# Turning the accumulated modulation of the second layer on VectorE instead of TensorE, each step tied behind its block

## The chip, the cores and the metric

One core of a Trainium2 chip runs the whole program in one launch. The metric is the device time of that launch in microseconds, as the median of several runs; one further run was profiled, and all rows below come from it.

## The reference, cut to what matters

Two layers of a trunk over 512 latent and 256 context tokens of width 1024, all in float32. Each layer first makes six vectors of 1024 (shift, scale and gate for two sub-layers) for the latent tokens and six for the context tokens:

```
mx = silu(c)     @ w_ada[i] + b_ada[i]      # latent,  6 * 1024 numbers
mc = silu(c_ctx) @ w_ada[i] + b_ada[i]      # context, 6 * 1024 numbers
sx1, ax1, gx1, sx2, ax2, gx2 = split(mx, 6) # the same for mc
h = rmsnorm(x) * (1 + ax1) + sx1            # then projection, conv, attention, merge
x = x + gx1 * merged
x = x + gx2 * (square(relu(modulate(rmsnorm(x)) @ w_mlp1[i])) @ w_mlp2[i])
```

`w_ada[i]` is 1024 x 6144. The two products with it are what the change is about, for layer 1 (the second). They depend on nothing in layer 0, so they can be made at any time before layer 1 starts.

## The kernel before, in words

Activations lie with the 1024 features on partitions (8 blocks of 128) and the 768 tokens along the free axis. Every float32 product is made as three products of a high and a low part (`mm3`, lines 107 to 111: high by high, low by high, high by low); `split` (line 75) makes the parts, the high one on ScalarE, the low one on VectorE or GpSimd. `fm_block` (line 113) makes one block of 128 output features for a group of tokens: 24 products, with 512 columns for a latent block and 256 for a context block. Weights come in slabs of 256 output columns (`load_slab`, line 84): one load on the SP queue, then the split. Two raw buffers and two of each part hold slabs in the second half of a layer; a slab serves two latent and two context blocks.

The stage around the change is the MLP of layer 0 (lines 1196 to 1294). Four chunks `cch` of 1024 hidden features follow each other. In each, `hidden` (line 1211) makes the blocks `f` from the normed input `h2h`, `h2l`: relu and square on ScalarE, then the low part `fl` by a subtraction on VectorE (line 1219). Then `out_slabs` (line 1153) makes the blocks `r` with the second weight, and `residual` (line 1137) adds each to the stream `X` on VectorE (line 1140), reading PSUM. Ahead of the MLP the same `out_slabs` made the output projection `o`, with a norm (`norm_mod`, line 305) after each half of the tokens: sums of squares, a product `nc_n`, a power on GpSimd, a diagonal `dg_n`, its product `nb_n` as broadcast, and then for each of eight feature blocks a product `nu_n` on VectorE, a shift on ScalarE (`h2h`) and a low part (`h2l`) on VectorE or GpSimd.

Layer 0 makes its own modulation with `ada_slab` (line 214), by products on TensorE in four column tiles. Layer 1's is made inside the MLP of layer 0 by the generator `ada_rows` (line 242). It goes over 24 pairs of steps; pair `s` makes 256 of the 6144 columns for both vectors. A step `n` has half of the 1024 rows in `ar`, a tile of 128 x 1024 numbers in the pool `araw` with one buffer, loaded on SP (line 247). The rows lie on partitions, so the sum over rows is first made over the four row blocks of a step with VectorE: a copy scaled by `cvec` on ScalarE for row block 0 (line 260), multiply-adds into the accumulator `a` of 128 x 512 for the others (line 263): six in an even step, eight in an odd one. Then the next load is issued, and the generator yields. After an odd step what is left is to add up the 128 partitions of `a`: four transposes on TensorE against the identity into a PSUM tile `adaps` (line 272), a reduce along the free axis on VectorE (line 275), which leaves 128 x 4 numbers, and the addition of `b_ada` (line 277) into `ad`. The accumulator comes from the tag `t2k` (four buffers), which the loads of `layer_params` use too.

`ada_step` (line 1205) moves the generator on by one step; a call of it is a tick below. It is called after each latent block of `f` (but for the last of a chunk, and, in the first chunk, only from the third slab on, since the first two slabs are walked in halves), and as `tick` after each latent block of `r`. Ahead of the last `out_slabs`, line 1238 runs what is left of it, and `ada_gain` (line 282) makes `A1` from columns 8 to 15 of `ad`. The PSUM tiles of latent blocks, of context blocks and of `adaps` come from pools of 2, 2 and 4.

What sets the order: the program is traced in the order of the code, and when it is built a planner gives each engine a fixed order of its instructions. It may move an instruction ahead of others when its inputs are ready earlier, as it did with the first steps of `ada_rows`. `tc.issue_after(ins)` ties the instructions traced inside it to stand behind `ins` on the engine of `ins`, and only those of that engine. The tag `dg` of `spool` (one buffer) is used for the diagonals of the norms and, in layer 0, by `ada_slab`.

Of the kernel before, what the change touches and what calls it, by code (L numbers as in the profile page):

```python
# [8 lines left out]
F32 = mybir.dt.float32  # L9
F32R = mybir.dt.float32r  # L10
AF = mybir.ActivationFunctionType
ALU = mybir.AluOpType
AX = mybir.AxisListType

P = 128
# [24 lines left out]
R_BADA, R_N1, R_N2, R_BG, R_BDW, R_LNG, R_LNB, R_ANG, R_C, R_CC, R_END = (  # L40
    0, 48, 56, 64, 80, 84, 88, 92, 93, 101, 109)
# [5 lines left out]
def f32(ap):  # L47
    return ap.bitcast(F32)
# [3 lines left out]
def trunk_kernel(  # L52
# [6 lines left out]
    nc = tc.nc  # L59
# [3 lines left out]
    cpool = ctx.enter_context(tc.tile_pool(name="cpool", bufs=1))  # L63
# [3 lines left out]
    spool = ctx.enter_context(tc.tile_pool(name="spool", bufs=2))  # L67
# [62 lines left out]
    nc.sync.dma_start(cst, consts[:, :C_COS])  # L130
    ident = cst[:, C_ID : C_ID + P]
    ones = cst[:, C_ONE : C_ONE + P]
    mhalf = cpool.tile([P, 8], F32, name="mhalf")
    nc.gpsimd.memset(mhalf, -0.5)

# [5 lines left out]
    state = {"behind": (), "turn": None}  # L141
# [100 lines left out]
    def ada_rows(i, L):  # L242


        def load(n):
            r = state["rp"].tile([P, KT // 2, 256], F32, tag="araw", bufs=1, name=f"ar{i}_{n}")
            nc.sync.dma_start(r, rows(w_ada[i], 256 * (n // 2), 256)[:, 4 * (n % 2) : 4 * (n % 2) + 4])
            return r

        r = load(0)  # L250
        for n in range(48):
            s = n // 2
            if n % 2 == 0:
                a = state["tp"].tile([P, 512], F32, tag="t2k", bufs=state["nt"], name=f"adaac{i}_{s}")
                a = a.rearrange("p (q n) -> p q n", q=2)
            for j in range(4):
                k = 4 * (n % 2) + j
                for q in range(2):
                    if k == 0:
                        nc.scalar.activation(out=a[:, q], in_=r[:, j], func=AF.Copy,  # L260
                                             scale=cvec[:, k, q : q + 1])
                    else:
                        nc.vector.scalar_tensor_tensor(  # L263
                            out=a[:, q], in0=r[:, j], scalar=cvec[:, k, q : q + 1], in1=a[:, q],
                            op0=ALU.mult, op1=ALU.add)
            if n < 47:
                r = load(n + 1)
            yield
            if n % 2:
                ps = state["mi"](f"adaps{i}_{s}")  # L270
                for m in range(4):
                    nc.tensor.transpose(ps[:, m * P : m * P + P],
                                        a[:, m // 2, m % 2 * P : m % 2 * P + P], ident)
                ad = L["ad"][:, :, 2 * s : 2 * s + 2]
                nc.vector.tensor_reduce(out=ad, in_=ps.rearrange("p (q m k) -> p q m k", q=2, m=2),
                                        axis=AX.X, op=ALU.add)
                nc.vector.tensor_tensor(
                    out=ad, in0=ad,
                    in1=L["cols"][:, R_BADA + 2 * s : R_BADA + 2 * s + 2].unsqueeze(1)
                    .to_broadcast([P, 2, 2]), op=ALU.add)  # L280

    def ada_gain(L, which, ks=slice(0, KT)):
        par, r0, nm = ((1, R_N1, "A1"), (4, R_N2, "A2"))[which]
# [72 lines left out]
    for t in range(NTT):  # L356
# [4 lines left out]
        if t == 1:  # L361
            L = layer_params(0)
# [17 lines left out]
    for t in range(NTT):  # L380
        xn = xns[t]
        nc.scalar.activation(out=xn, in_=xrs[t], func=AF.Square, accum_out=rs[:, t : t + 1])
        r = rs[:, t : t + 1]
# [9 lines left out]
    for s in range(2):  # L393
        nc.vector.tensor_tensor(
            out=cvec[:, :, s], in0=L["cols"][:, R_C + 8 * s : R_C + 8 * s + 8],
            in1=sg[:, 8 * s : 8 * s + 8], op=ALU.mult)
# [38 lines left out]
    for i in range(DEPTH):  # L435
# [5 lines left out]
        cols = L["cols"]  # L441
# [536 lines left out]
        for half, lst in ((1, ga), (0, gc)):  # L978
            for s in range(4):
# [6 lines left out]
                for m in range(2):  # L986
                    mb = 2 * s + m
                    t = g3(f"g{i}_{half}_{mb}")
                    lst[mb] = t
                    for g in groups:  # L990
                        W = g.stop - g.start
                        ps = ps_for(g, f"gt{i}_{half}_{mb}_{g.start}")
# [70 lines left out]
        for s in range(4):  # L1063
# [3 lines left out]
            for g in groups:  # L1067
                W = g.stop - g.start
                for m in range(2):
                    mb = 2 * s + m  # L1070
# [23 lines left out]
        for s in range(2):  # L1094
# [7 lines left out]
            for m in range(4):  # L1102
                mb = 4 * s + m
# [33 lines left out]
        def residual(mb, g, ps, gate):  # L1137
            W = g.stop - g.start
            s = int(g.start >= SEQ)
            nc.vector.scalar_tensor_tensor(  # L1140
                out=X[:, mb, g], in0=ps[:, :W], scalar=gate[:, s, mb : mb + 1], in1=X[:, mb, g],
                op0=ALU.mult, op1=ALU.add)

        def out_block(w, s, g, m, hidden, gate, nm, stats):
            mb = 2 * s + m
# [57 lines left out]
            hl = hpool.tile([P, KT, NT], F32R, tag="hl", name=f"h1l_{i + 1}")  # L1203

        def ada_step():
            if not last:
                next(ada_todo, None)

        for cch in range(4):
            fh, fl = [None] * KT, [None] * KT  # L1210
            def hidden(w, mb, m, g):
                W = g.stop - g.start
                ps = ps_for(g, f"f{i}_{cch}_{mb}_{g.start}")
                fm_block(ps[:, :W], w, m * P, lambda k: (h2h[:, k], h2l[:, k]), g)
                r = gp.tile([P, 512], F32, tag="ar", bufs=3, name=f"fr{i}_{cch}_{mb}_{g.start}")
                nc.scalar.activation(out=r[:, :W], in_=ps[:, :W], func=AF.Relu)
                nc.scalar.activation(out=fh[mb][:, g], in_=r[:, :W], func=AF.Square)
                nc.scalar.activation(out=r[:, :W], in_=r[:, :W], func=AF.Square)
                nc.vector.tensor_tensor(out=fl[mb][:, g], in0=r[:, :W], in1=f32(fh[mb][:, g]),
                                        op=ALU.subtract)  # L1220

            for mb in range(KT):
                fh[mb] = g3(f"fh{i}_{cch}_{mb}", F32R)
# [148 lines left out]
```

## Time and profile before

| what | value |
|---|---|
| median of 3 runs | 2361.62 us (2360.18 to 2363.51) |
| the profiled execution, whole | 2362.06 us |
| its span from first to last instruction | 2360.0 us |
| granted TensorE clock, mean | 0.987 |
| busy: TensorE, VectorE, ScalarE, GpSimd | 2288.2, 1468.9, 993.2, 684.2 us |
| chain of waits that ended last: TensorE, VectorE, ScalarE, GpSimd | 84%, 7%, 3%, 2% |

Shares are of the span. A busy time is the sum of an engine's instructions with overlaps counted once; TensorE's matmuls overlap each other, so the distance between two starts, not the duration of one, says what a matmul takes.

### The profile page before, as it was taken

The page shows a single profiled execution, that of the slowest core. Times are in us where ns is not written, and L with a number is a line of the kernel's source. Part 1 is how long each engine was busy: PE and PEld are TensorE (multiplying, and loading weights), DVE is VectorE, ACT ScalarE, POOL GpSimd, SP SyncE. Part 2 cuts the span into 40 slices and gives each one's busy share as a digit, 9 for nine tenths or more (in the row PEclk, how much of TensorE's full clock was granted, in tenths as well). Part 3 has the DMA queues.
Part 4 walks back from the last instruction along what each step waited for, and adds up shares of the span by engine and source line. Part 5 has one row for each costly group of instructions (what it writes and reads, how often), then busy time and mean ns, then how long its engine had stood idle before and what let it go on. Part 6 is the DMA issues. An engine that isn't in the chain of part 4 may idle for free.

```text
span 2360.0 us, 36545 instructions
## 1 busy us (share of the span) xinstructions
PE 2288.2 (97%) x14698; PEld 2051.8 (87%) x14698; DVE 1468.9 (62%) x2583; ACT 993.2 (42%) x1965; POOL 684.2 (29%) x790
## 2 busy tenths in 40 slices
PE   8999999999999999999999998999999999999999
PEld 6999998888888988888888998999877879888887
DVE  6777776699666675655463366776759975433332
ACT  5555654522332353342514345555542333432432
POOL 1866754100000133232322255766610000000000
PEclk9999999999999999999999999999999999999999
DMA  9211111144535223334332211111124324223322
GB/s 313 57 43 31 44 46 44 46 159 131 178 114 188 88 84 125 116 109 132 116 118 71 99 46 56 44 43 44 42 78 130 122 89 126 88 92 95 102 89 72
DMA packets 222570, 224.76 MB, mean 95 GB/s; under 512 B 6256, under 2 KB 212544, under 8 KB 222272
## 3 DMA queue, kind: packets, MB, share of 16 engines
q1 hardware_dynamic: 222400, 222.43, 29.5%
q8 instruction: 115, 1.88, 0.3%
q14 instruction: 55, 0.45, 0.1%
HBM read 208.73 MB, written 13.67 MB: 94 GB/s over the span
## 4 chain that ended last, share of the span: by engine, by line
PE 84%; DVE 7%; ACT 3%; POOL 2%; DMA 1%; issue 1%; SPq 0%; ACTq 0%; DVEq 0%; POOLq 0%
PE r L109 6%; PE r L110 6%; PE r L111 6%; PE f L110 6%; PE f L109 6%; PE f L111 6%; PE gt L109 3%; PE gt L111 3%; PE gt L110 3%; PE qk L109 2%; PE qk L110 2%; PE qk L111 2%; PE v L109 2%; PE v L110 2%; PE v L111 2%; PE o L111 2%
## 5 line engine op out<-in xcount | busy, mean ns | idle before, releaser
L110 PE MATMUL f<-h2l,h_w 128*128 128x512 f32 (+1 forms) x832 | 284.5, 343 | 3.6 <-DVE h2l L328 2.0
L109 PE MATMUL f<-h2h,h_w 128*128 128x512 f32 (+1 forms) x832 | 282.5, 344 | 2.0 <-ACT h2h L76 1.3
L109 PE MATMUL r<-fh,h_w 128*128 128x512 f32 (+1 forms) x832 | 283.9, 342 | 0.0
L110 PE MATMUL r<-fl,h_w 128*128 128x512 f32 (+1 forms) x832 | 283.0, 340 | 0.0
L111 PE MATMUL r<-fh,l_w 128*128 128x512 f32 (+1 forms) x832 | 282.9, 340 | 0.0
L111 PE MATMUL f<-h2h,l_w 128*128 128x512 f32 (+1 forms) x832 | 282.8, 342 | 0.0
L77 POOL TENSOR_TENSOR l_w<-r_w,h_w 128x1024 fp32r<-128x1024 f32 x64 | 156.7, 2471 | 346.9 <-ACT h_w L76 346.9
L76 ACT ACTIVATE h_w<-r_w 128x1024 fp32r<-128x1024 f32 x128 | 128.5, 1051 | 261.3 <-PE r L110 117.2
L263 DVE SCALAR_TENSOR_TENSOR adaac<-ar,cvec,adaac 128x256 f32<-128x256 f32 x336 | 176.7, 579 | 83.9 <-DMA ar<-in_w_ada_dram 62.0
L945 DVE SCALAR_TENSOR_TENSOR cacc<-z,cols,cacc 128x783 f32<-128x783 f32 (+1 forms) x240 | 201.4, 891 | 0.3
L109 PE MATMUL qk<-h_wqk,h1h 128*128 128x256 f32 x640 | 183.6, 289 | 2.1 <-ACT rw L542 1.4
L110 PE MATMUL qk<-l_wqk,h1h 128*128 128x256 f32 x640 | 180.7, 285 | 0.0
L110 PEld LDWEIGHTS f<-h2l,h_w 128*128 128x128 f32 x832 | 158.8, 191 | 22.7 <-POOL h2l L77 2.9
L111 PE MATMUL qk<-h_wqk,h1l 128*128 128x256 f32 x640 | 176.9, 285 | 0.2 <-POOL h1l L77 0.2
L712 DVE TENSOR_REDUCE st<-S 128x1 f32<-128x768 f32 (+1 forms) x160 | 134.7, 846 | 65.4 <-PE S L710 64.4
L1140 DVE SCALAR_TENSOR_TENSOR X<-r,ad,X 128x512 f32<-128x512 f32 (+1 forms) x104 | 64.8, 625 | 176.8 <-PE r L111 176.7
L109 PEld LDWEIGHTS f<-h2h,h_w 128*128 128x128 f32 x832 | 157.0, 191 | 20.4 <-ACT h2h L76 1.7
L111 PEld LDWEIGHTS f<-h2h,l_w 128*128 128x128 f32 x832 | 158.6, 191 | 17.7
L111 PEld LDWEIGHTS r<-fh,l_w 128*128 128x128 f32 x832 | 157.6, 190 | 17.8
L109 PEld LDWEIGHTS r<-fh,h_w 128*128 128x128 f32 x832 | 157.6, 190 | 17.2
L110 PEld LDWEIGHTS r<-fl,h_w 128*128 128x128 f32 x832 | 157.8, 190 | 16.9
L715 ACT ACTIVATE e<-S,st 128x768 f32<-128x768 f32 (+1 forms) x160 | 130.8, 820 | 36.6 <-DVE st L712 36.5
(253 smaller groups left out, 6240.4 us busy)
## 6 DMA issues: line engine op xcount, KB each, us to landing
r_w<-in_w_mlp_dram SPq DMA_DIRECT2D x64, 1024.0 KB, 5.5
ada<-in_w_ada_dram SPq DMA_DIRECT2D x24, 1024.0 KB, 5.4
ar<-in_w_ada_dram SPq DMA_DIRECT2D x48, 512.0 KB, 3.7
r_wqk<-in_w_in_dram SPq DMA_DIRECT2D x32, 512.0 KB, 5.4
r_wg<-in_w_in_dram SPq DMA_DIRECT2D x16, 1024.0 KB, 5.4
r_wv<-in_w_in_dram SPq DMA_DIRECT2D x8, 1024.0 KB, 5.3
r_wao<-in_w_attn_out_dram SPq DMA_DIRECT2D x8, 1024.0 KB, 5.4
r_wo<-in_w_out_dram SPq DMA_DIRECT2D x8, 1024.0 KB, 8.2
```

The source lines that it names most:

```text
L76: nc.scalar.activation(out=hi, in_=src, func=AF.Copy)
L77: return (lo_eng or nc.vector).tensor_tensor(out=lo, in0=src, in1=f32(hi), op=ALU.subtract)
L109: nc.tensor.matmul(ps, sh, mh, start=first, stop=False)
L110: nc.tensor.matmul(ps, sh, ml, start=False, stop=False)
L111: nc.tensor.matmul(ps, sl, mh, start=False, stop=last)
L263: nc.vector.scalar_tensor_tensor(out=a[:, q], in0=r[:, j], scalar=cvec[:, k, q : q + 1], in1=a[:, q], op0=ALU.mult, op1=ALU.add)
L712: nc.vector.tensor_reduce(out=st[:, m : m + 1], in_=S[:, :nkey], axis=AX.X, op=ALU.max, negate=True)
L715: nc.scalar.activation(out=e[:, :nkey], in_=S[:, :nkey], func=AF.Exp, bias=st[:, m : m + 1], accum_out=st[:, 2 + m : 3 + m])
L945: nc.vector.scalar_tensor_tensor(out=ca[cc][:, :CV], in0=zt[cc][:, t : t + CV], scalar=wcol, in1=ca[cc][:, :CV], op0=ALU.mult, op1=ALU.add)
L1140: nc.vector.scalar_tensor_tensor(out=X[:, mb, g], in0=ps[:, :W], scalar=gate[:, s, mb : mb + 1], in1=X[:, mb, g], op0=ALU.mult, op1=ALU.add)
```

## The change

After an odd step the accumulator is no longer turned by TensorE. VectorE turns it in blocks of 32x32 (each block in its place) into a second tile of the tag `t2k`, and a reduce along the free axis adds up the 32 numbers of each block's row. That leaves, for each of the four groups of 32 partitions, the sums over that group, in 16 columns of the tile `part`, which has room for eight pairs of steps and is taken from the tag `dg`. After every eighth pair (three times in all) `fold` adds the four groups by four products with `fold32`, a 128 x 32 matrix of four stacked identities made once at the start; each product writes 32 partitions of a PSUM tile. One VectorE addition with `b_ada` then writes 16 columns of `ad` for both vectors. The residual and the low part of `f` are remembered as they are traced, and each tick's VectorE instructions are tied behind the last one.

```diff
+    fold32 = cpool.tile([P, 32], F32, name="fold32")
+    nc.vector.tensor_reduce(out=fold32, in_=ident.rearrange("p (b r) -> p r b", b=4), axis=AX.X,
+                            op=ALU.add)
...
     def ada_rows(i, L):
+        def fold(s0):
+            ps = state["mi"](f"adaps{i}_{s0}")
+            for c_ in range(4):
+                nc.tensor.matmul(ps[32 * c_ : 32 * c_ + 32, :32], fold32, part[:, c_],
+                                 start=True, stop=True, tile_position=(0, 32 * c_))
+            nc.vector.tensor_tensor(
+                out=L["ad"][:, :, 2 * s0 : 2 * s0 + 16].rearrange("p q (n m) -> p n q m", n=8),
+                in0=ps[:, :32].rearrange("p (n q m) -> p n q m", n=8, q=2),
+                in1=L["cols"][:, R_BADA + 2 * s0 : R_BADA + 2 * s0 + 16]
+                .rearrange("p (n m) -> p n m", n=8).unsqueeze(2).to_broadcast([P, 8, 2, 2]),
+                op=ALU.add)
...
             if n % 2:
-                ps = state["mi"](f"adaps{i}_{s}")
-                for m in range(4):
-                    nc.tensor.transpose(ps[:, m * P : m * P + P],
-                                        a[:, m // 2, m % 2 * P : m % 2 * P + P], ident)
-                ad = L["ad"][:, :, 2 * s : 2 * s + 2]
-                nc.vector.tensor_reduce(out=ad, in_=ps.rearrange("p (q m k) -> p q m k", q=2, m=2),
-                                        axis=AX.X, op=ALU.add)
-                nc.vector.tensor_tensor(
-                    out=ad, in0=ad,
-                    in1=L["cols"][:, R_BADA + 2 * s : R_BADA + 2 * s + 2].unsqueeze(1)
-                    .to_broadcast([P, 2, 2]), op=ALU.add)
+                if s % 8 == 0:
+                    part = spool.tile([P, 4, P], F32, tag="dg", bufs=1, name=f"adp{i}_{s}")[:, :, :32]
+                b = state["tp"].tile([P, 512], F32, tag="t2k", bufs=state["nt"], name=f"adat{i}_{s}")
+                nc.vector.transpose(out=b, in_=a.rearrange("p q n -> p (q n)"))
+                nc.vector.tensor_reduce(
+                    out=part[:, :, 4 * (s % 8) : 4 * (s % 8) + 4].rearrange("p c n -> p n c"),
+                    in_=b.rearrange("p (n c r) -> p n c r", n=4, c=4), axis=AX.X, op=ALU.add)
+                if s % 8 == 7:
+                    fold(s - 7)
...
         def residual(mb, g, ps, gate):
-            nc.vector.scalar_tensor_tensor(
+            state["done"] = nc.vector.scalar_tensor_tensor(
                 out=X[:, mb, g], in0=ps[:, :W], scalar=gate[:, s, mb : mb + 1], in1=X[:, mb, g],
-                op0=ALU.mult, op1=ALU.add)
+                op0=ALU.mult, op1=ALU.add).ins
...
         def ada_step():
             if not last:
-                next(ada_todo, None)
+                with tc.issue_after(state["done"]):
+                    next(ada_todo, None)
...
-                nc.vector.tensor_tensor(out=fl[mb][:, g], in0=r[:, :W], in1=f32(fh[mb][:, g]),
-                                        op=ALU.subtract)
+                state["done"] = nc.vector.tensor_tensor(
+                    out=fl[mb][:, g], in0=r[:, :W], in1=f32(fh[mb][:, g]), op=ALU.subtract).ins
```

## Rows read from the trace of the kernel before

**Rows 1.** The page's first part: busy time, share of the span and instructions of each engine.
```profile
PE 2288.2 (97%) x14698; PEld 2051.8 (87%) x14698; DVE 1468.9 (62%) x2583; ACT 993.2 (42%) x1965; POOL 684.2 (29%) x790
```
**Rows 2.** Busy time by stretches: the stretch and its length in us, then busy us of each engine with its instructions, the granted clock, the DMA share and GB/s.
```profile
840.00:860.00 20.00, 17.23 (x113) 15.88 (x112) 13.81 (x35) 10.83 (x29) 4.34 (x6) 0.83 0.08 27
860.00:1310.00 450.00, 449.76 (x2637) 398.81 (x2636) 232.55 (x455) 158.41 (x273) 132.70 (x55) 1.00 0.35 113
```
**Rows 3.** Who TensorE waited for from 740 to 1380 us: us in total, times, longest.
```profile
PE f L110 <- DVE h2l L328: 2.0, 2, 1.8
PE adaps L272 <- DVE cols L164: 0.6, 1, 0.6
```
**Rows 4.** The transposes into the tile `adaps` from 860 to 1320 us: count, then ns shortest, median and longest, first and last start.
```profile
L272 PE MATMUL adaps<-cst,adaac x88: 270/272/277, 865.8 to 1310.9; 128*128 128x128 f32 x88
```
**Rows 5.** TensorE in order of time around one group of transposes: start, us, line, operation, count.
```profile
1059.52 0.40 PE L111 MATMUL r<-fh,l_w 128*128 128x512 f32 x1
1059.75 0.60 PE L272 MATMUL adaps<-cst,adaac 128*128 128x128 f32 x4
1060.11 0.48 PE L109 MATMUL r<-fh,h_w 128*128 128x512 f32 x1
1060.42 0.40 PE L110 MATMUL r<-fl,h_w 128*128 128x512 f32 x1
```
**Rows 6.** Busy time by stretches that reach from the first product of a slab to that of the next (columns as in rows 2): a slab without a group of transposes, and the next, with one.
```profile
1020.48:1037.13 16.65, 16.65 (x99) 14.76 (x98) 7.46 (x13) 8.06 (x14) 4.75 (x2) 1.00 0.40 127
1037.13:1054.27 17.14, 17.14 (x102) 15.14 (x101) 8.80 (x20) 4.03 (x7) 4.93 (x2) 1.00 0.29 92
```
**Rows 7.** TensorE in order of time, the products of one `ada_slab` in four column tiles.
```profile
24.83 1.07 PE L221 MATMUL adaps<-ada,cvec 128*32 128x256 f32 x16
```
**Rows 8.** TensorE in order of time at the first context block of `f`; in brackets the idle time before and what ended it.
```profile
849.02 0.66 PE L272 MATMUL adaps<-cst,adaac 128*128 128x128 f32 x4
850.25 0.66 PE L272 MATMUL adaps<-cst,adaac 128*128 128x128 f32 x4 [0.58 <-DVE cols L164]
850.66 0.48 PE L109 MATMUL f<-h2h,h_w 128*128 128x256 f32 x2
852.90 0.58 PE L110 MATMUL f<-h2l,h_w 128*128 128x256 f32 x1 [1.76 <-DVE h2l L328]
...
858.41 0.41 PE L111 MATMUL f<-h2h,l_w 128*128 128x256 f32 x1
...
858.97 0.28 PE L109 MATMUL f<-h2h,h_w 128*128 128x256 f32 x1
```
**Rows 9.** Busy time by stretches (columns as in rows 2): the stretch at the lower clock.
```profile
852.02:858.84 6.82, 5.74 (x25) 5.44 (x26) 6.60 (x17) 2.81 (x7) 2.25 (x3) 0.50 0.12 36
```
**Rows 10.** Groups of VectorE's instructions from 848.6 to 858.5 us: count, busy us and mean ns, and the idle time before them.
```profile
L320 DVE SCALAR_TENSOR_TENSOR nu_n<-X,A,nb_n 128x256 f32<-128x256 f32 x8 | 3.5, 473 | 1.6 <-PE nb_n L302 1.6
L263 DVE SCALAR_TENSOR_TENSOR adaac<-ar,cvec,adaac 128x256 f32<-128x256 f32 x6 | 2.8, 472 | 0.0
L275 DVE TENSOR_REDUCE ad<-adaps 128x4 f32<-128x512 f32 x2 | 1.4, 676 | 0.0
```
**Rows 11.** ScalarE in order of time at the same place.
```profile
848.91 0.89 ACT L260 ACTIVATE adaac<-ar,cvec 128x256 f32<-128x256 f32 x2
...
850.01 0.49 ACT L324 ACTIVATE h2h<-nu_n,ad 128x256 fp32r<-128x256 f32 x1
```
**Rows 12.** Operations of VectorE over the whole span. The first three: count, busy us, mean ns, idle before. The last, from the view of one line: count, ns shortest, median and longest.
```profile
L275 DVE TENSOR_REDUCE ad<-adaps 128x4 f32<-128x512 f32 x24 | 16.4, 685 | 27.4 <-PE adaps L272 27.4
L277 DVE TENSOR_TENSOR ad<-ad,cols 128x4 f32<-128x4 f32 x24 | 5.9, 247 | 0.1
L414 DVE TENSOR_SCALAR XN<-XN,A,ad 128x512 f32<-128x512 f32 x8 | 4.3, 543 | 0.1
...
L263 DVE SCALAR_TENSOR_TENSOR adaac<-ar,cvec,adaac x336: 467/477/2637, 765.0 to 1251.3; 128x256 f32<-128x256 f32 x168
```
**Rows 13.** One pair of steps in a calm slab, on ScalarE and VectorE in order of time, and how long the loads of `ar` took from issue to landing.
```profile
1094.67 0.91 ACT L260 ACTIVATE adaac<-ar,cvec 128x256 f32<-128x256 f32 x2 [3.98 <-PE adaps L272]
...
1096.37 1.67 DVE L263 SCALAR_TENSOR_TENSOR adaac<-ar,cvec,adaac 128x256 f32<-128x256 f32 x4
...
1101.95 2.46 DVE L263 SCALAR_TENSOR_TENSOR adaac<-ar,cvec,adaac 128x256 f32<-128x256 f32 x6 [1.05 <-DMA ar<-in_w_ada_dram]
...
1104.73 0.87 DVE L263 SCALAR_TENSOR_TENSOR adaac<-ar,cvec,adaac 128x256 f32<-128x256 f32 x2
...
DMA to landing us min/median/max: 3.4/3.7/9.0
```
**Rows 14.** An odd step on VectorE and the split of a slab on GpSimd beside it.
```profile
954.59 6.34 DVE L263 SCALAR_TENSOR_TENSOR adaac<-ar,cvec,adaac 128x256 f32<-128x256 f32 x8 [1.83 <-DMA ar<-in_w_ada_dram]
...
953.34 4.93 POOL L77 TENSOR_TENSOR l_w<-r_w,h_w 128x1024 fp32r<-128x1024 f32 x2 [12.50 <-ACT h_w L76]
```
**Rows 15.** What the SP queue waited for from 800 to 1380 us: us in total, times, longest.
```profile
SPq L247 <- DVE adaac L263: 247.8, 42, 28.0
```
**Rows 16.** One weight slab: its load on SP, its split on ScalarE, and from the page's part on DMA issues the size and us to landing of such loads.
```profile
1094.60 0.37 SPq L90 DMA_DIRECT2D r_w<-in_w_mlp_dram  x1
...
1122.98 2.01 ACT L76 ACTIVATE h_w<-r_w 128x1024 fp32r<-128x1024 f32 x2 [1.53 <-PE f L110]
...
r_w<-in_w_mlp_dram SPq DMA_DIRECT2D x64, 1024.0 KB, 5.5
```

## The prediction, made before the changed kernel was run

> **What bounds the kernel now.** I read the page first: TensorE is busy 97% of the span, VectorE 62% [rows 1]. That share is an average, so next came the table by stretches. From 860 to 1310 us, the MLP of layer 0 in which every step of `ada_rows` but the first few runs, TensorE is busy 449.76 of 450.00 us at the full granted clock and VectorE 232.55 [rows 2]. In this stretch an instruction taken off TensorE is time taken off the end, and VectorE has 217 us to spare. Just ahead of it, 840 to 860 us, TensorE is busy 17.23 of 20.00 us at a granted clock of 0.83 [rows 2]: the one bad place of the stage. The waits name it: 1.8 us for `h2l` of VectorE and 0.6 us in the `adaps` transposes [rows 3]. So there are two prices to find: what a group of four transposes costs TensorE, and what the steps do to that bad place.
>
> **Term 1, the transposes.** All 24 groups go (L272); 88 of the 96 transposes, 22 groups, run inside or right at the end of the full stretch [rows 4]. A matmul's 272 ns is no price, since matmuls overlap; starts are. Around one group they are 1059.52 (product before), 1059.75 (group), 1060.11 and 1060.42 (two products after) [rows 5]. From 1059.52 to 1060.42 are 0.90 us; the first product took 0.23 of them, a second one is another 0.23, so a group costs 0.44. A second way: a slab of weights (two latent and two context blocks) without a group takes 16.65 us, the next one, with a group, 17.14 [rows 6], a difference of 0.49. I take 0.45: 22 x 0.45 = 9.9 us gained (ends 9.7 and 10.8). The last two groups stand at the bad place and belong to term 3.
>
> **Term 2, the products that replace them.** Three folds of four 32-column products. The trace has the same shape of product in `ada_slab`: sixteen, four column tiles each, with 256 moving columns, take 1.07 us, so 0.27 for a set of four [rows 7]. A fold moves 32 columns. Ends: nothing, and 0.45 as for a group of transposes. I take 0.27, the nearest row: 3 x 0.27 = 0.8 us lost.
>
> **Term 3, the bad place.** In order on TensorE: two groups of transposes from 849.02 and, after a wait, 850.25; the first context block of `f` from 850.66; 1.76 us idle until `h2l` is there at 852.90; then products of 0.41 us each, until at 858.97 they take 0.28 again [rows 8]. The granted clock was 0.50, the 1.2 GHz level, from 852.02, within the idle time, to 858.84 [rows 9]. Why was `h2l` late? VectorE was never idle between 849 and 858, and of its work there 2.8 + 1.4 = 4.2 us were ada steps (six L263 and two L275) standing among the eight `nu_n` and the `h2l` [rows 10]. ScalarE ran two `adaac` copies, 0.89 us, right ahead of the norm's `h2h` [rows 11]. After the change no step's VectorE work can be here: the first tick comes behind the `fl` of a latent block of the third slab, and this is a context block of the first, ahead of it. The L260 pair goes with it, since its slab of rows needs the steps before it through the one `araw` buffer. So the norm's chain ends up to 4.2 us earlier. Against that, TensorE loses filler (the two groups) and still waits for a chain of some 5 us, so a low stretch may stay: a block that is over by about 855 and a clock at 0.50 until about 858 would give back half of those 3 us. Ends: 4.2 gained, and 3.4 lost (a second low stretch of 6.82 us at half rate). I take 2.5 gained: 4.2 with no low clock, some 2.7 with it, and a little under both, since the ScalarE part of the chain gets only 0.9 back.
>
> **What costs nothing, and what hides it.** On VectorE each slab loses an L275 (0.68) and an L277 (0.25) [rows 12] and gets a turn and a reduce of 128x512. No row shows a turn. Its bounds: 0.54, the one-source 128x512 operation in L414, and 2.6, the longest that an operation was held in L263 [rows 12]; I take 0.68, the reduce of the same size. That is 24 x (1.36 - 0.93) = 10 us more (at the bound of 2.6, 56 us), under 217 idle; without that cover it would be the full 10. `fold32` is one small reduce at the start, behind the constants that TensorE's first transposes need as well; at most one such reduce, 0.4 us, and it is hidden by the loads of `x`.
>
> The Trainium skill (VectorE: DVE Perf Modes, Rules for kernel authors) speaks against the edit: it sends a 128x128 transpose to TensorE if PSUM will do as its target, and calls the reduce the slowest operation of VectorE. No run here shows a block turn yet; by its figure of 311 ns for a turn in bf16 four of them would be an estimated 1.2 us a slab and the sum would stay where it is, since rows of this trace put the price on the idle engine.
>
> **The steps that move.** Each issues one load of `araw` on SP, two `adaac` copies on ScalarE if even, and six or eight L263; only the VectorE part is tied to its block, now behind a latent block's residual or low part and ahead of the context blocks' ones. Those wait up to 6.3 us more, and nobody is near them: their PSUM tiles are two deep and a slab lasts 16.65 us. Per slab two steps follow each other through the one buffer. In a calm slab the even one takes 3.4 us (1094.67 to 1098.04), the odd one 3.7 (1101.95 to 1105.60) and each load 3.7 [rows 13], with the turn and reduce 1.4: 15.9 us, just under the slab. Beside a split on GpSimd an odd step took 6.34 [rows 14], so 18.5. Such stretches make the steps late against their blocks by 1.9 us a slab. What is queued behind: SP holds each load until the step before has read the buffer, 247.8 us of waiting in 42 waits already [rows 15], and weight slabs are issued behind it. A slab's load was issued at 1094.60 and first split at 1122.98 [rows 16]; with 5.5 us to land that leaves 22.9 us. So I cost the move at nothing. The steps that ran from 765.0 us on now start some 100 us later, and the last one, from before 1251.3 [rows 12] to about 1300 (an estimate: the last group of transposes, where line 1238 is traced, stands at 1310.9 [rows 4]); its columns are needed only in layer 1, and `A1` hangs on the first fold.
>
> **Sum.** 2362.06 us (the profiled execution, span 2360.0 and 2.06 around it) - 9.9 + 0.8 - 2.5 = 2350.5. The median of the runs lies 0.44 below that execution, so 2350.0.
>
> **Rivals.**
> *The bad place stays bad* (or the tie binds nothing there): with less filler TensorE idles longer, the clock falls as before, term 3 is nothing: 2352.5. With a second low stretch, 3.4 lost: 2355.9. For it: the low stretch follows idle time [rows 8, 9], and this idle time is a norm's chain that stays. Against it: 4.2 us of other work leave that chain.
> [...]
> *The folds wait on TensorE.* The order on each engine is fixed when the program is built; a fold placed ahead of a late turn stops TensorE, as `h2l` did. Three waits of 1.8 [rows 3] and one low stretch, 3.4 (half of 6.82 [rows 9]): 2350.0 + 8.8 = 2359, no change that can be told. Against it: 22 groups of the old kind stood in the same queue behind the same engine and the 450 us have 0.24 us idle.
> *Slower: the steps throttle the weights.* If each of the 24 slabs takes 18.5 us of steps, SP falls behind by 24 x 1.9 = 46 us; it decides from the point where the 22.9 us of slack are used, so 23 us come through: 2350 + 23 = 2373. For it: the long odd steps. Against it: later slabs had none.
>
> **How the numbers follow.** Forecast 0.63, bad place stays 0.20, folds wait 0.10, throttled 0.05, more gain than the ends 0.02. A measurement of this kernel tells from about 0.2%, 4.7 us: faster is below 2356.9. The first two and the last make faster 0.85, the third same 0.10, the fourth slower 0.05. The range: at the low side 10.8 + 4.2 with free folds, 2346.6, and the runs' own 1.5 below; at the high side the bad place with a second low stretch and the runs' 1.9: 2345 to 2358. It leaves out the last two rivals.
>
> **What would show it.** Right: no L272 group; slabs of 16.6 to 16.7 us throughout; three sets of four small products with under 0.5 us between their neighbours; `f` of the first context block at full rate before 857. Wrong: TensorE waits ahead of a fold or for weights (`h_w`), slabs over 17 us, or a turn over 2.6 us. A kernel as fast as before with those slabs would mean the end is set elsewhere.

## The result, and the profile after

The changed kernel takes 2350.64 us (median of 6 runs, 2348.48 to 2354.14), the kernel before, run beside it, 2362.57 (6 runs, 2360.18 to 2368.32): a ratio of 0.9943 [0.9931, 0.9955], 11.9 us faster. The forecast was 2350.0. The number was met within 0.6 us, in part by luck: terms 1 and 3 gained 3.7 us more than forecast, and the folds lost 4.2 us more.

The profiled execution of after took 2353.61 us, near the top of its runs, with a span of 2351.8. Its lines of the changed code: 252 the products of `fold`, 254 the addition behind them, 276 the scaled copy, 279 the multiply-adds, 289 the turn, 290 the reduce, 1154 `residual`, 1235 the low part `fl`, 312 `dg_n`, 316 `nb_n`.

The page's first part, beside [rows 1]: TensorE has 72 instructions fewer and is busy 11.6 us less, VectorE 7.1 us more.

```profile
PE 2276.6 (97%) x14626; PEld 2042.8 (87%) x14626; DVE 1476.0 (63%) x2587; ACT 995.2 (42%) x1965; POOL 687.3 (29%) x790
```

Busy time by stretches (columns as in rows 2): the bad place, the MLP, two slabs, and a stretch at the lower clock.

```profile
840.00:860.00 20.00, 18.97 (x149) 17.87 (x149) 8.19 (x22) 13.16 (x32) 5.87 (x6) 1.00 0.01 2
860.00:1300.00 440.00, 437.71 (x2533) 387.93 (x2532) 253.40 (x495) 157.62 (x271) 131.44 (x54) 1.00 0.38 121
1162.56:1165.97 3.41, 3.41 (x18) 3.41 (x17) 1.91 (x5) 1.22 (x3) 0.00 (x0) 0.50 0.41 123
929.51:946.17 16.66, 16.66 (x98) 14.77 (x97) 9.06 (x21) 2.92 (x4) 4.75 (x2) 1.00 0.42 127
946.17:962.83 16.66, 16.66 (x98) 14.77 (x97) 9.68 (x22) 2.92 (x4) 4.75 (x2) 1.00 0.40 126
```

Against [rows 2] the bad place is cured further than forecast: 1.03 us idle where it was 2.77, and the granted clock is 1.00 where [rows 9] had 6.82 us at 0.50, the 1.2 GHz level. Two slabs in a row take 16.66 us, where [rows 6] had 16.65 and 17.14; the others that lie wholly in the MLP take as long, but for two, 17.09 with the first fold and 20.91 with the second. The MLP has 2.29 us of idle time that was not there, and a low stretch behind it.

Who TensorE waited for from 740 to 1380 us (us in total, times, longest), to be read against [rows 3]:

```profile
PE adaps L252 <- DVE adp L290: 2.3, 1, 2.3
PE nb_n L316 <- DVE dg_n L312: 1.8, 1, 1.8
PE f L109 <- ACT h2h L76: 0.5, 1, 0.5
PE f L110 <- POOL h2l L77: 0.3, 1, 0.3
```

The waits in the first context block of `f`, in order of time, answer to [rows 8]: 0.47 and 0.32 us where one wait was 1.76, and 0.28 us a product right behind them.

```profile
852.34 0.50 PE L109 MATMUL f<-h2h,h_w 128*128 128x256 f32 x2 [0.47 <-ACT h2h L76]
853.16 0.39 PE L110 MATMUL f<-h2l,h_w 128*128 128x256 f32 x1 [0.32 <-POOL h2l L77]
853.38 0.28 PE L111 MATMUL f<-h2h,l_w 128*128 128x256 f32 x1
```

The new operations (count, ns shortest, median and longest, first and last start):

```profile
L289 DVE STREAM_TRANSPOSE adat<-adaac x24: 694/703/712, 887.8 to 1295.6; 128x512 f32<-128x512 f32 x24
L290 DVE TENSOR_REDUCE adp<-adat x24: 678/688/691, 889.2 to 1296.3; 128x16 f32<-128x512 f32 x24
L252 PE MATMUL adaps<-adp,fold x24: 189/196/217, 1015.2 to 1300.9; 128*32 128x32 f32 x24
```

**Where the time goes.** The products of `f`, `r`, `v` and the rest are the same in both kernels, so the start of the n-th of them can be compared (worked out from the two traces; the time is that of before, minus is earlier):

| at (us) | after | after, profiled again (exp. 10) | fold later (exp. 3) |
|---|---|---|---|
| 803.3, in `o` | +0.79 | -1.04 | +1.17 |
| 861.9, past the bad place | -4.86 | -5.18 | -4.49 |
| 868.6, in the MLP | -5.30 | -5.63 | -4.93 |
| 1168.5, `f`, ahead of the second fold | -11.09 | -11.42 | -10.72 |
| 1174.3, `r`, behind the second fold | -6.84 | -7.29 | -10.72 |
| 1413.4, `v` of layer 1 | -10.75 | -11.18 | -14.19 |
| end of the span | -8.2 | -12.5 | -10.8 |

So the norm ahead of the MLP gave 5.65 us (4.1 in the second profile of the same kernel); 0.4 of either is only that four small products `nc_n` of the norm stand just ahead of the point at 803.3 us in after and behind it in before. The groups of transposes between 868.6 and 1168.5 us gave about 6 (less one fold), and the second fold took over 4 back. Behind 1413 us nothing was changed; there the executions differ among themselves: the stretches at 0.50 add up to 34.1 us in layer 1 of the first profile of after, 23.9 in the second and 30.7 in before, and a little under half of such a stretch is lost (term 3, below).

### The profile page after: what moved, and what is told of

Same layout as the page of the kernel before. It is cut to its first block, busy times and chain, and to the rows that moved or that the text cites. A ratio compares the mean times of both kernels' runs of the same rounds, so it can differ in the third digit from the quotient of the medians.

```text
span 2351.8 us, 36393 instructions
## 1 busy us (share of the span) xinstructions
PE 2276.6 (97%) x14626; PEld 2042.8 (87%) x14626; DVE 1476.0 (63%) x2587; ACT 995.2 (42%) x1965; POOL 687.3 (29%) x790
## 4 chain that ended last, share of the span: by engine, by line
PE 83%; DVE 7%; ACT 4%; POOL 2%; DMA 2%; issue 1%; SPq 0%; ACTq 0%; POOLq 0%; DVEq 0%
PE r L109 6%; PE r L110 6%; PE r L111 6%; PE f L110 6%; PE f L109 6%; PE f L111 6%; PE gt L109 3%; PE gt L110 3%; PE gt L111 3%; PE qk L109 2%; PE qk L110 2%; PE qk L111 2%; PE v L109 2%; PE v L110 2%; PE v L111 2%; PE o L109 2%
## 5 line engine op out<-in xcount | busy, mean ns | idle before, releaser
L279 DVE SCALAR_TENSOR_TENSOR adaac<-ar,cvec,adaac 128x256 f32<-128x256 f32 x336 | 160.8, 541 | 44.6 <-DMA ar<-in_w_ada_dram 22.7
L1235 DVE TENSOR_TENSOR fl<-fr,fh 128x512 fp32r<-128x512 f32 (+1 forms) x104 | 67.9, 659 | 138.4 <-ACT fr L1234 138.2
```

The source lines that it names most:

```text
L279: nc.vector.scalar_tensor_tensor(out=a[:, q], in0=r[:, j], scalar=cvec[:, k, q : q + 1], in1=a[:, q], op0=ALU.mult, op1=ALU.add)
L1235: state["done"] = nc.vector.tensor_tensor(out=fl[mb][:, g], in0=r[:, :W], in1=f32(fh[mb][:, g]), op=ALU.subtract).ins
```

## The experiments

Each diff is against the changed kernel unless it says otherwise. The kernel before ran beside each one; ratios are against it. Two theories stood at first: that the transposes taken off TensorE bring the gain and the tie only helps, and, as its rival, that the tie, which keeps the steps out of the norm, brings most of it.

**1. The turn without the tie.**

```diff
-                with tc.issue_after(state["done"]):
-                    next(ada_todo, None)
+                next(ada_todo, None)
```

> The turn, the reduce and the folds as changed, without the tie (ticks call the generator without issue_after). Theory (two separate parts: transposes off TensorE, some 9.4 us net; the tie, which empties the norm stage of ada work, some 5 us): ratio to before 0.9960 to 0.9985, and the trace shows L263-type multiply-adds between 845 and 860 us, a wait of TensorE for h2l there and a granted clock of 0.5 after it. Rival (the norm stage was freed by the missing transposes, the tie does nothing): ratio as for the whole change, 0.994, and no low clock between 845 and 865 us.

Measured: 2387.4 us, 1.0091 [1.0073, 1.0109], slower than before. At the bad place the first theory holds: nine multiply-adds stand between 845 and 862 us, TensorE waits 1.7 and 2.3 us there, the granted clock is 0.50 for 10.24 us, and from 803.3 to 861.9 us the products lose 1.9 us on before where those of after gain 5.65.

```profile
851.95:862.19 10.24, 7.85 (x34) 7.56 (x35) 8.50 (x21) 3.62 (x9) 3.57 (x4) 0.50 0.16 51
```

The rest of the loss neither theory had. TensorE's waits, 740 to 1400 us:

```profile
PE r L109 <- DVE X L1154: 13.4, 4, 7.8
PE f L109 <- DVE X L1154: 3.9, 4, 1.9
```

The longest of them, VectorE and then TensorE in order of time:

```profile
1233.60 2.22 DVE L279 SCALAR_TENSOR_TENSOR adaac<-ar,cvec,adaac 128x256 f32<-128x256 f32 x1
1239.65 4.21 DVE L279 SCALAR_TENSOR_TENSOR adaac<-ar,cvec,adaac 128x256 f32<-128x256 f32 x4 [3.83 <-DMA ar<-in_w_ada_dram]
1243.79 0.74 DVE L1154 SCALAR_TENSOR_TENSOR X<-r,ad,X 128x512 f32<-128x512 f32 x1
```
```profile
1236.59 0.28 PE L111 MATMUL r<-fh,l_w 128*128 128x256 f32 x1
1244.67 0.76 PE L109 MATMUL r<-fh,h_w 128*128 128x512 f32 x1 [7.81 <-DVE X L1154]
```

The residual that frees a PSUM tile stands on VectorE behind multiply-adds that wait for their load, and TensorE stands 7.81 us for the tile. VectorE's order is fixed, so an instruction that VectorE has idle time for still costs TensorE whatever stands behind it and comes late. How late residuals start behind the last product of their block, from 860 to 1312 us (worked out from the traces, median and longest, us): before 0.04 and 10.2, after 0.04 and 1.9, this kernel 9.97 and 19.7. So two things could hold the multiply-adds that the planner puts ahead: the load through the one buffer, or the splits on GpSimd. Experiment 6 asks which.

**2. The tie alone**, put on the kernel before (with the two lines that remember `state["done"]`, as in the change).

```diff
         def ada_step():
             if not last:
-                next(ada_todo, None)
+                with tc.issue_after(state["done"]):
+                    next(ada_todo, None)
```

> The kernel before with the tie alone; the 24 groups of four transposes stay on TensorE. Theory: the norm stage up to 870 us gains some 5 us and nothing else moves, so about 2357.5 against 2362.5, ratio 0.9970 to 0.9990, with the low clock near 855 us gone. Rival (tie worthless by itself): ratio 0.9995 to 1.0005. A third reading (the tie costs, since a group of transposes then waits for a late step on TensorE): ratio over 1.001 with waits of TensorE for adaac.

Measured: 2366.87 us, 1.0005 [0.9990, 1.0020]: no difference, the rival's number. But two large ones are inside it, the theory's gain and the third reading's wait. From 803.3 to 861.9 us its products move from +1.67 to -2.43 (-2.87 at 868.6), so the tie alone mends the bad place by 4.1 us, as much as the second profile of the whole change. From 1151 to 1168.5 they move from -0.35 to +5.08:

```profile
PE adaps L272 <- DVE adaac L263: 4.6, 2, 3.5
```

The tie makes the accumulator late, and transposes that stand in TensorE's queue wait for it, with a low clock behind. The tie pays only where TensorE no longer stands behind the steps, and the turn (experiment 1) only with the tie.

**3. The fold one tick later**, so that its reduce has long ended.

```diff
-                if s % 8 == 7:
-                    fold(s - 7)
+                if s == 23:
+                    fold(16)
+            elif n and s % 8 == 0:
+                fold(s - 8)
```

> The whole change, but the first two folds are traced one tick later, after the next even step, so that their products cannot stand on TensorE ahead of a reduce that waits for a load. Theory (the wait of 2.3 us and the low clock of 3.4 us at half rate behind it, at the second fold, are in most executions): 4 us less than the change, some 2346.5, ratio to before 0.9925 to 0.9935, no wait of TensorE for adp. Rival (the wait is an accident of the profiled execution): as the change, ratio 0.994 and over.

Measured: 2348.45 us, 0.9922 [0.9905, 0.9940]. The wait for `adp` is gone and TensorE is never idle in the MLP:

```profile
860.00:1300.00 440.00, 440.00 (x2569) 389.90 (x2568) 264.11 (x498) 160.25 (x276) 132.37 (x55) 1.00 0.39 121
```

From 1168.5 to 1413 us its products gain 3.5 us on before where those of after lose 0.3: the 3.8 us that the wait and the low stretch behind it cost. The intervals of the two kernels overlap; experiments 10 and 11 repeat both.

**4. The change, with the transposes made all the same**, unread, from the accumulator.

```diff
+                pu = state["mi"](f"adunread{i}_{s}")
+                for m in range(4):
+                    nc.tensor.transpose(pu[:, m * P : m * P + P],
+                                        a[:, m // 2, m % 2 * P : m % 2 * P + P], ident)
```

> The whole change, and in addition the 24 groups of four transposes of the accumulator into a PSUM tile that nothing reads. Theory (a group costs TensorE 0.45 us in a stage that it fills): 24 x 0.45 = 10.8 us more than the change, some 2361.4, ratio to before 0.9985 to 1.0000. Rival (the gain came from order and waits, the transposes were hidden): within 2 us of the change, ratio 0.993 to 0.995.

Measured: 2376.29 us, 1.0037 [1.0019, 1.0055], 0.0094 or 22 us above the change where 24 groups at 0.45 are 10.8. A wait comes on top:

```profile
PE adunread L290 <- DVE adaac L279: 7.6, 5, 2.9
```

10.8 for the groups, 7.6 of waiting and some 3.0 for 6.8 us at the lower clock in the MLP are 21.4, of which the change's own wait and low stretch (3.8, below) have to go off, since this kernel has no wait for `adp`: 17.6. Counted by the products, it loses 17.8 us on the change from 868.6 to 1413 us; the rest of the 22 arises behind that point, where the kernels are the same. So this doesn't price the transposes: those of a tied accumulator cost nearly twice their own time.

**5. Transposes that wait for nobody**: experiment 3 with 24 groups of transposes of a constant, unread, tied behind the product traced last.

```diff
+                pu = state["mi"](f"adunread{i}_{s}")
+                with tc.issue_after(state["mm"].ins):
+                    for m in range(4):
+                        nc.tensor.transpose(pu[:, m * P : m * P + P], ones, ident)
```

> The kernel with the fold one tick later, and in addition 24 groups of four transposes of a constant into a PSUM tile that nothing reads, each tied behind the last product of its latent block on TensorE, so that they never wait for VectorE. Theory (the price of a group by itself is 0.45 us; what the unread transposes of the accumulator cost above that was waiting): 24 x 0.45 = 10.8 us more than without them, ratio to before 0.9955 to 0.9980, no wait of TensorE for these products. Rival (the group costs far more than its starts show, as the 25 us suggested): ratio 1.000 and over. Second rival (hidden): 0.991 to 0.994.

Measured: 2362.86 us, 0.9982 [0.9971, 0.9993], 0.0060 or some 14 us above experiment 3 (0.0035 or 8 us above its repetition, experiment 11), just more than the band that was expected. No wait for them shows, they are there 96 times, and TensorE is as full as before:

```profile
L291 PE MATMUL adunread<-cst x96: 270/272/273, 888.8 to 1311.3; 128*128 128x128 f32 x96
860.00:1310.00 450.00, 449.76 (x2650) 398.19 (x2650) 245.01 (x495) 161.07 (x277) 132.32 (x54) 1.00 0.38 119
```

From 868.6 to 1413 us experiment 3 gains 9.3 us on before, this one loses 1.4: 10.7 us for 24 groups, 0.45 each. Term 1 is what the transposes cost by their own time on TensorE.

**6. No tie, with two buffers of half the size for the loads**, so that a load is under way while another is read (a second full buffer has no room).

```diff
-            r = state["rp"].tile([P, KT // 2, 256], F32, tag="araw", bufs=1, name=f"ar{i}_{n}")
+                t_ = state["rp"].tile([P, KT // 4, 256], F32, tag="araw", bufs=2, name=f"ar{i}_{n}_{q_}")
...
-                with tc.issue_after(state["done"]):
-                    next(ada_todo, None)
+                next(ada_todo, None)
```

> The turn without the tie, with each step's load of araw in two halves in two buffers of half the size, so that the first half of the next step loads while the second half of this one is read. Theory (without the tie the residual stands behind multiply-adds that wait for their load): the waits of TensorE for X of 13.4 us shrink to under 4, ratio to before 0.994 to 1.001 instead of 1.009. Rival (what holds the residual is the collision of the multiply-adds with the splits on GpSimd, not the load): ratio 1.005 to 1.010, waits for X as long as before.

Measured: 2382.74 us, 1.0066 [1.0050, 1.0082]. VectorE's waits for the loads, over the whole span, first in experiment 1, then here (the line moved), and behind them TensorE's wait for `X`, 740 to 1400 us, here:

```profile
DVE adaac L279 <- DMA ar<-in_w_ada_dram: 71.4, 23, 4.1
```
```profile
DVE adaac L283 <- DMA ar<-in_w_ada_dram: 33.3, 34, 2.3
PE r L109 <- DVE X L1158: 17.8, 6, 4.9
```

Less than half of the load waiting is left, and the residuals are as late as in experiment 1 (median 10.5 us, longest 19.4). So less waiting for the load makes the residual no earlier; the tie does (0.04 us in after), which changes the order, in which a step's multiply-adds otherwise stand ahead of it. The number is the rival's, but its reason is not shown: that those multiply-adds are stretched by the splits (2.6 us instead of 0.48, [rows 12]) fits; it was not taken away by itself.

**7. Every turn made twice**, on experiment 3.

```diff
                 nc.vector.transpose(out=b, in_=a.rearrange("p q n -> p (q n)"))
+                nc.vector.transpose(out=b, in_=a.rearrange("p q n -> p (q n)"))
```

> The kernel with the fold one tick later and every turn made twice into the same tile, 24 x 0.7 = 17 us more on VectorE. Theory (VectorE's idle time covers it once the residuals stand ahead): as without it, ratio to before 0.991 to 0.994, no new wait of TensorE. Rival (the steps are at their limit, as in the version without the tie): ratio 0.996 and over, with waits of TensorE for X or adp.

Measured: 2371.87 us, 1.0023 [1.0005, 1.0041], 0.010 or 24 us above experiment 3 (18 above its repetition), for 17 us more on an engine with 176 us idle in the MLP (the row of experiment 3): the rival's number and its wait. Counted by the products, the MLP loses 19.2 us on experiment 3, and 18.1 of them between 1288 and 1320 us, at the last fold, the one that is not put off: 12.6 of waiting for it, 2.1 just ahead of it for ScalarE, and some 3.1 for 7.1 us of work at 0.50. The waits, the stretch around them and VectorE ahead of the fold:

```profile
PE adaps L252 <- DVE adp L291: 12.6, 1, 12.6
PE f L109 <- ACT fr L1235: 2.1, 1, 2.1
1300.00:1330.00 30.00, 17.40 (x128) 17.14 (x128) 16.48 (x27) 8.51 (x17) 7.27 (x3) 0.73 0.28 88
```
```profile
1306.97 6.36 DVE L279 SCALAR_TENSOR_TENSOR adaac<-ar,cvec,adaac 128x256 f32<-128x256 f32 x8 [2.92 <-DMA ar<-in_w_ada_dram]
1313.37 0.71 DVE L289 STREAM_TRANSPOSE adat<-adaac 128x512 f32<-128x512 f32 x1
1314.12 0.71 DVE L290 STREAM_TRANSPOSE adat<-adaac 128x512 f32<-128x512 f32 x1
```

The steps, not VectorE, are full: load, copy, multiply-adds and turn of two steps follow each other through one buffer within a slab of 16.66 us. With 0.71 more a slab they lag their blocks: the first turn starts at 888.8 us here and at 888.1 in experiment 3, the last pair at 1313.4 and the last turn there at 1292.1.

```profile
L289 DVE STREAM_TRANSPOSE adat<-adaac x24: 700/704/714, 888.1 to 1292.1; 128x512 f32<-128x512 f32 x24
```

What lags at the end stops TensorE.

**8 and 9. The wait for `dg_n`.** The diagonal of a norm is made by ScalarE, in 8 for all norms, in 9 for the one ahead of this MLP alone; both on experiment 3.

```diff
-            nc.vector.tensor_scalar(dg[:, t, :], ident, ms[:, t : t + 1], None, ALU.mult)
+            nc.scalar.activation(out=dg[:, t, :], in_=ident, func=AF.Copy, scale=ms[:, t : t + 1])
```

> The kernel with the fold one tick later, and the diagonals of the norms made on ScalarE instead of VectorE, where GpSimd's splits held two of them for 2.4 us each at 823 us in the changed kernel. Theory: the wait of TensorE for dg of 1.8 us goes, and one norm chain less is late: 1 to 3 us less than without, ratio to before 0.9905 to 0.9920. Rival (ScalarE is in the middle of a split there and is as late): 0.992 to 0.994.

> The fold one tick later, and the diagonals on ScalarE only in the norm ahead of layer 0's MLP, where the wait for dg stood; all other norms as before. Theory (in the version with all diagonals on ScalarE the MLP stage gained 2 us more and later norms lost it): 2 us less than with the fold alone, ratio to before 0.990 to 0.992. Rival (what was lost later came from another order of layer 1, not from the later diagonals): 0.993 to 0.995.

Measured: 2353.13 us, 0.9942 [0.9926, 0.9958], and 2350.85 us, 0.9941 [0.9928, 0.9954]: the rivals' numbers or next to them. But not for the first rival's reason: the wait of 1.8 us is gone in both. In 9 the part from 803 to 868.6 us gains 8.1 us instead of 6.1, and the end shows none of it; in 8 the lead of 16.87 us at 1288 is down to 7.4 at the end, with 44.4 us at the lower clock in layer 1. What takes it back in 9 is within what layer 1 differs by from one execution to the next, and stays open.

**10 and 11. The change, and experiment 3, once more**, side by side.

> The changed kernel once more, beside the next one on the same chip, since their intervals overlap so far. Theory (the wait of the second fold is in most executions): ratio to before 0.9935 to 0.9950, and over the next one's by 0.0015 to 0.0025. Rival (accident): within 0.0005 of the next one.

> The fold one tick later once more. Theory: ratio to before 0.9915 to 0.9930. Rival: as the change beside it.

Measured: 2352.19 us, 0.9946 [0.9931, 0.9962], and 2350.80 us, 0.9947 [0.9932, 0.9961]. The second profile of the change has the same wait, and experiment 11 again has none:

```profile
PE adaps L252 <- DVE adp L290: 2.3, 1, 2.3
```

So the wait belongs to the order of the kernel and putting the fold off removes it, twice out of two. Over 12 runs each the means are 2351.4 and 2349.7 us; the ratios beside each other are the same. The number is the rival's, its reason (an accident) is not what the profiles show. Whether the 3.8 us that they show arrive at the end is not settled by these runs, and no version tried is clearly faster than the change.

## Why the prediction was right, and where it was not

**Term 1, forecast -9.9: right.** From 868.6 to 1168.5 us 13 groups of before are gone and one fold of 0.4 us is there: 5.79 + 0.4 = 6.2 us, 0.48 a group, so 10.5 for 22; experiment 5 puts it at 0.45. Both lie between the ends given.

**Term 2, forecast +0.8: mis-sized, by a misread row.** TensorE in order of time at the third fold:

```profile
1300.59 0.28 PE L111 MATMUL f<-h2h,l_w 128*128 128x256 f32 x1
1300.80 0.27 PE L252 MATMUL adaps<-adp,fold 128*32 128x32 f32 x8
1300.99 0.39 PE L109 MATMUL r<-fh,h_w 128*128 128x256 f32 x1
1301.21 0.28 PE L110 MATMUL r<-fl,h_w 128*128 128x256 f32 x1
1301.33 0.28 PE L111 MATMUL r<-fh,l_w 128*128 128x256 f32 x1
```

From 1300.59 to 1301.33 are 0.74 us, of which three products at 0.12 are 0.36: 0.38 for the fold (0.41 at the first one), 1.2 for three. The four products of the code stand as eight records. So do those of [rows 7]: sixteen records are the eight products of one `ada_slab`, as its count over the whole span of before says, 384 for 24 slabs of eight:

```profile
L221 PE MATMUL adaps<-ada,cvec x384: 379/379/632, 20.3 to 733.9; 128*32 128x256 f32 x192
```

The prediction read sixteen products and four sets in 1.07 us, 0.27 each; it is two sets, 0.53 each. Read rightly the row was an upper bound, and 0.4, with 32 columns in place of 256, lies under it.

**Term 3, forecast -2.5, ends -4.2 and +3.4: mis-sized, at one profile beyond its end.** The shift at 861.9 against 803.3 us is 5.65 in one profile and 4.1 in the other (5.2 and 3.7 without the four `nc_n`). The mis-sized step is "4.2 with no low clock". It priced the gain by how much VectorE work leaves the norm's chain, and took the clock only as a deduction from that. The price has to be taken on TensorE. In before, at 0.50 and at 1.00:

```profile
854.14 0.41 PE L109 MATMUL f<-h2h,h_w 128*128 128x256 f32 x1
854.35 0.41 PE L110 MATMUL f<-h2l,h_w 128*128 128x256 f32 x1
859.09 0.28 PE L110 MATMUL f<-h2l,h_w 128*128 128x256 f32 x1
859.21 0.28 PE L111 MATMUL f<-h2h,l_w 128*128 128x256 f32 x1
```

At the lower clock a product starts 0.21 us behind the one before, at the full one 0.12: 44% of such time is lost. Between the two points idle time went from 3.6 us to 2.9, two groups left, 1.1 by their starts, the `nc_n` are the 0.4, and the products of `f` took 3.4 less, some 2.5 of it because 25 of them no longer stand at the lower clock (44% of the 5.74 us that TensorE works there [rows 9]): 5.6 in all, and nearly half of it from the clock that was expected to fall again. The two profiles differ by the clock as well. TensorE waits 1.8 us for `dg_n` in both; behind that wait the second one (first row) ran at 0.50, the first one (second row) did not:

```profile
826.95:830.36 3.41, 3.41 (x18) 3.41 (x17) 3.17 (x8) 1.50 (x4) 0.00 (x0) 0.50 0.87 268
828.30:831.70 3.40, 3.40 (x27) 3.35 (x28) 2.71 (x8) 2.19 (x6) 0.24 (x1) 1.00 0.73 217
```

Its products of `f` take 1.5 us more, the whole difference. The gain of this part is the tie's, as the prediction had it (the tick comes too late to be there): the tie alone gives 4.1, with such a low stretch (experiment 2), and without it 1.9 are lost (experiment 1).

The Trainium skill (TensorE: Matmul & The Clock Gate, Terms) prices the gate by the time spent at the lower rate times the share of pulses lost, half. The trace shows a little less, the 44% above. The prediction's 3.4, half of 6.82 [rows 9], also took in 1.1 us in which TensorE waited; 2.5 is what the rows show.

**"The folds wait on TensorE" (0.10): it happened, at one fold of three.** VectorE, then TensorE, at the second one:

```profile
1156.69 0.69 DVE L289 STREAM_TRANSPOSE adat<-adaac 128x512 f32<-128x512 f32 x1
1160.28 0.88 DVE L279 SCALAR_TENSOR_TENSOR adaac<-ar,cvec,adaac 128x256 f32<-128x256 f32 x2 [2.90 <-ACT adaac L276]
1161.09 0.68 DVE L290 TENSOR_REDUCE adp<-adat 128x16 f32<-128x512 f32 x1
```
```profile
1159.34 0.28 PE L110 MATMUL f<-h2l,h_w 128*128 128x256 f32 x1
1161.91 0.27 PE L252 MATMUL adaps<-adp,fold 128*32 128x32 f32 x8 [2.29 <-DVE adp L290]
```

The planner put two multiply-adds of the next step between turn and reduce; they wait for a ScalarE copy, the copy for its load, and VectorE sits idle 2.90 us with the reduce ready behind them. TensorE loses 2.29, and then 1.5 of the 3.41 us at 0.50: 3.8, and so say the products (4.25 from 1168.5 to 1174.3 us, with 0.4 for the fold itself). The argument against this rival, that 22 groups had stood in that queue unharmed, was about untied steps; the tie made them later (experiments 2 and 4). Put together with these sizes, 10.5 + 5.65 - 1.2 - 3.8 are 11.1 us from 803 us on; 11.5 were measured (+0.79 to -10.75). The forecast was 11.6: 3.7 us of gain too little in terms 1 and 3, and 4.2 of loss too little at the folds. That they nearly cancel is luck.

**"What costs nothing": the number was right, the reason wrong.** The turn took 0.703 us (0.68 taken) and stayed hidden. But it is hidden by the step's place within its slab, not by 217 us of idle VectorE: with the turn doubled 18 to 24 us come through (experiment 7), and the same work in another order costs 1.0091 where the change has 0.9943, 35 us (experiment 1). The lag of 1.9 us a slab that the prediction worked out was the right thing to fear, only on the wrong queue: it asked how late the weights get, and not who else stands behind the steps on VectorE or TensorE. TensorE never waits for `h_w` in this stretch, so "the steps throttle the weights" did not happen.

On the turn itself, the estimate from the Trainium skill (VectorE: DVE Perf Modes, The three transpose paths) of 1.2 us a slab is not what was measured; 0.703 is, for 128x512 in float32, and the measurement decides.

**"The bad place stays bad": no.** The clock was 1.00 from 840 to 860 us, and with the tie it was so in every profile; the low stretch that some of them have lies ahead of it, behind the wait for `dg_n`.

**What would show it.** Right: no L272, and the context block at full rate behind its waits, from 853.4, ahead of 857. Half right: slabs of 16.66 us, but not throughout, and three sets of four, of which two stand close between their neighbours. Of the signs of a wrong forecast two came true, both at the folds: TensorE's wait ahead of the second one, and slabs over 17 us (17.09 and 20.91).

## What to carry to other kernels

Idle time on an engine hides new work only if no one behind it in that engine's fixed order is waited for: for an edit ask first what stands behind the added or moved instruction, and what they wait for, and only then how much idle time there is. An operation moved off the bounding engine is worth its start-to-start time there, and can lose part of that again if what is left of it on that engine reads something fresh (here 3.8 of 10.5 us): let it read one tick later. Price a bad place by what the bounding engine loses in it, its idle time and what its work at the lower clock takes longer (here 0.21 us a product instead of 0.12), not by the work that you take out of the chain that it waits for.

## What the runs showed of the hardware

The same wait is not always followed by the lower clock. Eight profiles (after, experiments 2 to 5, 7, 10 and 11) have TensorE's wait of 1.8 us for `dg_n`; behind it the granted clock was 0.50 for 3.41 us in four of them (2, 5, 7 and 10) and 1.00 in the others.

A VectorE operation with one source and one number per partition can be held beside a split on GpSimd as the multiply-adds are [rows 14]. GpSimd's split and VectorE's two `dg_n`, in order of time in after:

```profile
823.33 4.72 POOL L77 TENSOR_TENSOR l_w<-r_w,h_w 128x1024 fp32r<-128x1024 f32 x2
823.40 4.73 DVE L312 TENSOR_SCALAR dg_n<-cst,ms_n 128x128 f32<-128x128 f32 x2 [0.88 <-POOL ms_n L309]
```

Each of the two takes 2.4 us, as long as one instruction of the split, where it takes 0.28 elsewhere. The turn did not show this: three turns in all the profiles stood beside an instruction of over 1 us on GpSimd (one each in experiments 1, 6 and 7) and took 0.70 to 0.71 us, as the others. Three are few; in the change itself no turn met one.

The Trainium skill (SBUF — State Buffer, Summary: rules for kernel authors) has it that, when VectorE works in a mode that takes two ports, or reads two inputs from SBUF while the GpSimd operation reads SBUF, the one of the two that begins second stands until the other is done. The start of `dg_n` 0.07 us behind the split and its 2.4 us agree; in which mode it ran, no row shows.
